# The last output projection: forms loaded as they stand in DRAM, half of it added to the residual by transfers, the last norm's rows fetched one product earlier

## The chip, the cores and the metric

The kernel runs on one core of a Trainium2 chip. The metric is the time of one execution in device microseconds (us), lower is better. Engines: PE (TensorE) multiplies matrices, ACT (ScalarE) and DVE (VectorE) work on elements, POOL (GpSimd) and SP (SyncE) issue transfers (DMAs). Sixteen DMA engines do the transfers of all queues. POOL issues the accumulating ones, which add to what stands at the target.

## The reference

Two layers on x of 512 rows x 2048 columns, all float32. The change is in the end of the second layer:

```python
def retention_branch(x, w_in, w_out):
    proj = jnp.einsum('bsd,de->bse', x, w_in)
    q, k, v, gate = jnp.split(proj, [...], axis=-1)
    ...                                   # rotary, chunkwise retention, 8 heads
    o = group_norm_heads(o).reshape(B, S, RET_V_WIDTH)      # 4096 wide
    y = o * jax.nn.silu(gate)
    return jnp.einsum('bse,ed->bsd', y, w_out)              # (4096, 2048)

    for i in range(DEPTH):                # layer 0: fox_branch, layer 1: retention_branch
        ...
        h = layer_norm(DEEPNORM_ALPHA * h + y, ln_gain[i], ln_bias[i])
```

## The kernel before

Products are taken with a scheme of seven products for eight quarter blocks (p1 to p7), on sums and differences of quarters. The activations' seven **forms** are called a11, a12, a22, s1, s2, s3, s4; `FORM` says which product uses which. The weights' sums are made on DVE (`w_q`, line 577). Each operand is split into a rounded part h (ACT, line 307) and the rest l (DVE, line 308), and a product is three matmuls (lines 312 to 314).

A **unit** is one projection of 1024 columns by 2048 rows of weights: 7 products of 4 blocks for a wide one, each block 12 matmuls. The last output projection is four units: 14 and 15 multiply the first 2048 of the 4096 columns of y, 16 and 17 the second 2048. `ORDER` and `EARLY` (unit 17) give the order of the products.

The program order on every engine is planned when the kernel is built, by the class `Order`. It goes from block to block (a **slot**; the planner counts 2.72 us for it) and lets **tasks** (generators) take steps between blocks. A step yields `need(...)`: its cost in DVE and ACT time, what it waits for, and tiles from rings, for instance `tmp=2`. Tasks of a lower rank come first. `give("tmp", 3)` returns a tile three slots later. The ring `tmp` has four tiles of 128 x 512.

The parts that the change touches:

- `retain()` is the end of a head. For the last head (7) its last loop makes four outputs y and -y, each in two `tmp` tiles, and `give_forms` (line 828) stores or accumulates them into the forms in DRAM, `yf[i]` (y_a, y_s in the profile). Then `given[1]` counts the head. It has rank 2.
- `fetch_forms` loads the forms of half i (1 for units 14 and 15, 2 for units 16 and 17) into `y_raw` and splits them. The loads wait for `given[1] >= 4 * i`. `fetch_while(2)` starts it while unit 15 runs: a11 when p5 is done, s1 when p6 is done, and so on.
- `residual` has written `ALPHA` times the first layer's normed result (gain and bias applied) to `z_res` in DRAM, 16 pieces of 128 x 512. `add_half` takes the sums of units 14 and 15: `loads_of` loads a piece of `z_res` into a `tmp` tile (line 1448, rank 1), DVE adds the unit's sum (line 1862), POOL stores it as `z_half` (line 1863). Units 16 and 17 load `z_half` and add their own sums (`add_z`, line 1472).
- A unit's sums stand in **kept** tiles (`keep`, line 425, copied out of PSUM by ACT): `hand` passes them on, for (0, 0), (0, 1) and (1, 1); the sum (1, 0) is passed on while it stands in its PSUM bank x. `after` has the additions and subtractions at products' ends (lines 460, 465, 470).
- `last_gains` fetches the last norm's gain and bias, each row of 512 spread over 128 partitions, 8 transfers of POOL (line 1885), one step each. In unit 17 POOL also accumulates weights (`v_sum`, line 493, after SP's load; `w_q`, line 613).

Of the kernel before, what the change touches and what calls it, by code (L numbers as in the profile page):

```python
# [11 lines left out]
F32 = mybir.dt.float32  # L12
F32R = mybir.dt.float32r
I32 = mybir.dt.int32
AF = mybir.ActivationFunctionType
ALU = mybir.AluOpType

P = 128
# [3 lines left out]
ST = S // P  # L22
# [36 lines left out]
EARLY = (("p1",), ("p5",), ("p2", "p6"), ("p3",), ("p7",), ("p4",))  # L59
# [30 lines left out]
class Order:  # L90
# [17 lines left out]
    def give(self, ring, after=0):  # L108
        if after:
            self.later.append((self.now + after, ring))  # L110
        else:
            self.free[ring] += 1
# [7 lines left out]
    def spawn(self, steps, rank=2):  # L120

        task = dict(steps=steps, last=self.now - 1, rank=rank)
        try:
            task["need"] = next(steps)
        except StopIteration:
            return
        at = sum(t["rank"] <= rank for t in self.tasks)
        self.tasks.insert(at, task)
# [99 lines left out]
def need(dve=0.0, act=0.0, pe=0.0, wait=1, until=lambda: True, **rings):  # L228
    return dict(dve=dve, act=act, pe=pe, wait=wait, until=until, rings=rings)
# [3 lines left out]
def trunk(ctx: ExitStack, tc: tile.TileContext, xq, x, fb_f, columns, wf_in, narrow, wide, ln_g, ln_b, rot, decay,  # L233
          out):
    nc = tc.nc
    home = dict(HOME)
    pool = ctx.enter_context(tc.tile_pool(name="sb", bufs=1))
    psum = ctx.enter_context(tc.tile_pool(name="ps", bufs=1, space=bass.MemoryType.PSUM))
    dram = ctx.enter_context(tc.tile_pool(name="dr", bufs=1, space=bass.MemoryType.DRAM))
    o = Order()  # L240
    spawn, take, give, free, require = o.spawn, o.take, o.give, o.free, o.require

    def f32(t):
        return t.bitcast(F32)
# [4 lines left out]
    def sb2(name):  # L249
        return pool.tile([P, 512], F32, name=name, tag="tmp", bufs=4)  # L250

    def tmp(name):
        take("tmp")
        return sb2(name)
# [50 lines left out]
    def split(src, h, l):  # L305

        nc.scalar.activation(h, src, AF.Copy)  # L307
        nc.vector.tensor_sub(l, src, f32(h))  # L308
# [8 lines left out]
    forms, ready = {}, {}  # L317

    def new_form(name):
        forms[name] = [pool.tile([P, 8, 256], F32R, name=name, tag=t) for t in home[name]]  # L320
        ready[name] = set()

    def split_form(name, src, k0, k1, es=slice(None), whole=True):
        split(src, *(t[:, k0:k1, es] for t in forms[name]))
        if whole:
            ready[name].update(range(k0, k1))
# [14 lines left out]
    def join_room():  # L341
        yield need(until=lambda: "room" in stock and free["y0"])
        stock.remove("room")
        take("st")
        take("y0")
        give("g2")
# [418 lines left out]
    def combine(rest, plain):  # L765
# [41 lines left out]
        for c in range(2):  # L807
# [7 lines left out]
    yf = [{f: dram.tile([P, 8, 256] if i == 0 else [P, 2, 8, P], F32, name=f"y_{f}{i}")  # L815
           for f in (("a11", "a12", "a21", "a22") if i == 0 else FORM.values())} for i in range(3)]
    z_norm = [dram.tile([P, D], F32, name=f"z_norm{s}") for s in range(ST)]
    z_res = {(s, c): dram.tile([P, 512], F32, name=f"z_res{s}{c}") for s in range(ST) for c in range(4)}
    z_half = {(s, c): dram.tile([P, 512], F32, name=f"z_half{s}{c}") for s in range(ST) for c in range(4)}


    given = [0, 0]
# [22 lines left out]
    VIA = {"a11": "s1", "s1": "s2", "s2": "s4", "s4": "s3", "s3": "a12", "a12": "a22"}  # L845
    passing = set()

    def fetch_forms(i, names):

        at = {}  # L850

        def loads():
            for n in names:
                if n not in VIA:
                    yield need(g0=1)
                    take("g0")
                t = pool.tile([P, 8, 256], F32, name="y_raw", tag=home[VIA[n]][0] if n in VIA else "g0")
                passing.add(VIA.get(n))
                for c in (0, 4):
                    yield need(wait=2, until=lambda: given[1] >= 4 * i)  # L860
                    for e in range(2):
                        nc.sync.dma_start(t[:, c:c + 4, e * P:(e + 1) * P], yf[i][n][:, e, c:c + 4])
                    at[n, c] = t, o.now

        spawn(loads(), 0)
        for n in names:
            for c in (0, 4):
                yield need(dve=1.14, act=0.97,
                           until=lambda: n not in passing and (n, c) in at and o.now - at[n, c][1] >= 4)
                if c == 0:  # L870
                    new_form(n)
                split_form(n, at[n, c][0][:, c:c + 4], c, c + 4)
            passing.discard(VIA.get(n))
            if n not in VIA:
                give("g0")

    def fetch_while(i):

        take = lambda *names: lambda: spawn(fetch_forms(i, names))
        return {"p5": take("a11"), "p6": take("s1"), "p7": take("s2", "s4"), "p4": take("s3", "a12", "a22")}  # L880
# [93 lines left out]
    class Pair:  # L974
# [13 lines left out]
        def take(self, m, n, tile, done):  # L988
            def copy():
                yield need(act=0.5, until=self.has_room)  # L990
                if self.raw is None:
                    self.new_raw()
                    self.new_sums()
                nc.scalar.activation(self.raw[m][:, :, n * 256:(n + 1) * 256], tile, AF.Copy)
                yield need(act=1.2)
                self.squares(m, n, tile, 0)
                done()
                self.have += 1

            spawn(copy(), 0)  # L1000
# [403 lines left out]
    def two_banks():  # L1404
# [5 lines left out]
        BOTH, then={len(BOTH) // 2 - 1: lambda: spawn(fetch("a21", "k2", "k0", "k1")), len(BOTH) - 1: late})  # L1410
# [28 lines left out]
    def loads_of(src, u, order, held):  # L1439

        got = {}

        def steps():
            for m, n in ORDERS[order]:
                for e in range(2):
                    yield need(tmp=1, until=lambda: len(got) < held and given[0] == FH)
                    t = tmp("z_in")
                    nc.sync.dma_start(t, src(2 * m + e, 2 * u + n))
                    got[m, n, e] = t, o.now

        return got, steps
# [128 lines left out]
    def last_banks():  # L1580
# [4 lines left out]
    sink, steps = add_z(0, ALPHA, x_rows, "plain", 2)  # L1585
    Plain(wide, 4, sink, last_banks).run(
        HELD, then={8: lambda s=steps: spawn(s(), 1)})
# [6 lines left out]
    sink, steps = add_z(1, ALPHA, x_rows, "each")  # L1594
# [249 lines left out]
    for h in heads[1:]:  # L1844
        if h.h == 2:
            spawn(biases())
        h.qk_unit.run(then={"p3": lambda h=h: spawn(h.attend())})
        then = fetch_while(1) if h.h == RH - 1 else {}
        last = then.get("p4", lambda: None)
        h.vg_unit.run(SLOW if h.h == 1 else ORDER, leaves=h.h == RH - 1,  # L1850
                      then={**then, "p4": lambda h=h, last=last: (spawn(h.retain()), last())})


    def add_half(u, held):
        got, steps = loads_of(lambda s, c: z_res[s, c], u, "order", held)

        def sink(m, n, tile, done):
            def add():
                for e in range(2):
                    yield need(dve=0.6, until=lambda: (m, n, e) in got and o.now - got[m, n, e][1] >= 2)  # L1860
                    t, _ = got.pop((m, n, e))
                    nc.vector.tensor_add(t, t, tile[:, e])
                    nc.gpsimd.dma_start(z_half[2 * m + e, 2 * u + n], t)
                    give("tmp", 3)
                done()

            spawn(add(), 0)

        return sink, steps

    sink, steps = add_half(0, 2)
    Unit(wide, 14, sink, u2="in1", p1="y0").run(then={"p6": lambda s=steps: spawn(s(), 1)})
    sink, steps = add_half(1, 2)
    Unit(wide, 15, sink, u2="k2").run(leaves=True, then={0: lambda s=steps: spawn(s(), 1), **fetch_while(2)})

    gb = []

    def last_gains():
        for i in range(2):
            gb.append(pool.tile([P, D], F32, name="ln_last", tag=home["a11"][i]))  # L1880
        for c in range(4):
            cs = slice(c * 512, (c + 1) * 512)
            for t, src in zip(gb, (ln_g, ln_b)):
                yield need()
                nc.gpsimd.dma_start(t[:, cs], src[1:2, cs].to_broadcast([P, 512]))

    def biases_there():

        yield need()
        nc.gpsimd.dma_start(row_b[0:1, 0:1], bf[0:1, :])  # L1890
        yield need(wait=4)
        nc.gpsimd.dma_start(bf[0:1, :], row_b[0:1, 0:1])
        yield need(wait=4)
        nc.vector.tensor_copy(bf[0:1, :], bf[0:1, :])
        fox["biased"] = True
# [26 lines left out]
    def last_stores(s):  # L1922
# [3 lines left out]
        for c in (0, 1, 3, 2):  # L1926
# [6 lines left out]
            else:  # L1933
                nc.gpsimd.dma_start(out[s * P:(s + 1) * P, cs], z, accum_op=ALU.add)

    half = lambda s, c: z_half[s, c]
    spawn(join_room(), 0)
    sink, steps = add_z(0, 1, half, "order")
    Unit(wide, 16, sink, u2="k2").run(then={0: lambda s=steps: spawn(s(), 1)})
    sink, steps = add_z(1, 1, half, "early")  # L1940
    Unit(wide, 17, sink, u2="k2").run(EARLY, then={0: lambda s=steps: (spawn(s(), 1), spawn(biases_there(), 0)), "p2": lambda: spawn(last_gains(), 0),
                                          "p3": lambda: [spawn(x) for x in (first_stores(), last_stores(2), last_stores(3))]}, last=True)
    o.flush()
    require(lambda: not o.tasks)
# [51 lines left out]
```

## Time and profile before

| what | us |
|---|---|
| median of 3 runs | 2376.63 |
| lowest and highest of them | 2374.23, 2378.85 |
| the profiled execution's own time | 2375.62 |
| its span, first to last instruction | 2373.9 |
| PE busy | 2305.4 |
| DVE busy | 1893.7 |
| ACT busy | 1214.0 |
| POOL busy | 166.0 |

The span is 1.7 us shorter than the execution's own time, as it leaves out what lies around the instructions. Lines of the profile name the engine, the line of the kernel and out<-in by the program's names; "PEld" is PE's load of weights, "SPq" SP's queue. Matmuls overlap, and their ends are modelled, so PE's busy time is a little too high.

### The profile page before, as it was taken

To read this page: it belongs to the slowest core of one execution; us is meant where nothing else is said; L and a number is where in the kernel's file an instruction comes from. 1 tells how busy PE (TensorE), PEld (TensorE's weight loads), DVE (VectorE), ACT (ScalarE), POOL (GpSimd) and SP (SyncE) were. 2 spreads that over 40 slices of the span, in tenths; PEclk is the share of its full clock that TensorE was granted. 3 is DMA by queue.
4 is the path that set the end of the run, shared out by engine and by line. 5 is a ranking of instruction groups with operands and counts; after the bars stand their busy time and mean duration, and the time that the engine had idled before them with its cause. 6 is when DMAs were issued, how large, how long until landed. Compare 5 with 4: busy or idle time off the path is not lost.

```text
span 2373.9 us, 32923 instructions
## 1 busy us (share of the span) xinstructions
PE 2305.4 (97%) x12424; PEld 1972.5 (83%) x12424; DVE 1893.7 (80%) x2477; ACT 1214.0 (51%) x1762; POOL 166.0 (7%) x256
## 2 busy tenths in 40 slices
PE   9999999989999999999999999999999999999995
PEld 9878778779899778888889898988888898777784
DVE  5887777777865655679889888888888889987977
ACT  4556656556554534565444545454545445554533
POOL 0000000000000000010010101010101001011002
PEclk9999999999999999999999999999999999999998
DMA  6355555455644457675585758575656659689778
GB/s 225 123 199 197 164 179 182 160 178 175 200 153 147 134 195 253 222 191 151 208 257 211 250 178 233 183 200 198 214 182 203 210 169 272 212 266 297 238 248 187
DMA packets 186350, 477.36 MB, mean 201 GB/s; under 512 B 18224, under 2 KB 63424, under 8 KB 185680
## 3 DMA queue, kind: packets, MB, share of 16 engines
q1 hardware_dynamic: 160288, 399.48, 50.2%
q0 software_dynamic: 25904, 75.78, 12.6%
q8 instruction: 97, 1.59, 0.3%
q14 instruction: 61, 0.50, 0.1%
HBM read 415.39 MB, written 64.00 MB: 202 GB/s over the span
## 4 chain that ended last, share of the span: by engine, by line
PE 61%; DVE 7%; DMA 4%; ACT 3%; issue 3%; SPq 0%; POOL 0%; DVEq 0%; ACTq 0%; POOLq 0%
PE acc L312 18%; PE acc L313 18%; PE acc L314 18%; DVE w_l L308 3%; DMA w_raw<-in_wide 2%; ACT w_h L307 2%; PE mmp L312 1%; PE mmp L313 1%; PE mmp L314 1%; DVE w_q L577 1%; PE mmp L1277 1%; DMA v_sum<-in_wide 1%; PE mmp L1800 1%; DMA y_raw<-y_a 0%; PE mmp L1132 0%
## 5 line engine op out<-in xcount | busy, mean ns | idle before, releaser
L307 ACT ACTIVATE w_h<-w_q 128x1024 fp32r<-128x1024 f32 x360 | 380.7, 1059 | 427.7 <-DVE w_q L577 229.6
L312 PE MATMUL acc<-w_h,a 128*128 128x512 f32 (+1 forms) x1440 | 535.5, 372 | 7.3 <-DVE kept L470 5.2
L308 DVE TENSOR_TENSOR w_l<-w_raw,w_h 128x1024 fp32r<-128x1024 f32 x314 | 383.6, 1222 | 190.8 <-ACT w_h L307 189.6
L313 PE MATMUL acc<-w_l,a 128*128 128x512 f32 (+1 forms) x1440 | 528.8, 367 | 5.2 <-DVE w_l L308 5.1
L314 PE MATMUL acc<-w_h,a 128*128 128x512 f32 (+1 forms) x1440 | 528.2, 367 | 0.0
L308 DVE TENSOR_TENSOR w_l<-w_q,w_h 128x1024 fp32r<-128x1024 f32 x360 | 439.6, 1222 | 107.4 <-ACT w_h L307 100.8
L307 ACT ACTIVATE w_h<-w_raw 128x1024 fp32r<-128x1024 f32 x314 | 331.8, 1058 | 363.2 <-PE acc L314 171.6
L313 PE MATMUL acc<-w_l,s 128*128 128x512 f32 (+1 forms) x1280 | 487.4, 381 | 9.8 <-DVE w_l L308 9.7
L312 PE MATMUL acc<-w_h,s 128*128 128x512 f32 (+1 forms) x1280 | 490.7, 383 | 0.4 <-ACT w_h L307 0.4
L314 PE MATMUL acc<-w_h,s 128*128 128x512 f32 (+1 forms) x1280 | 485.8, 380 | 0.0
L312 PEld LDWEIGHTS acc<-w_h,a 128*128 128x128 f32 x1440 | 272.0, 189 | 53.8 <-issue 9.6
L313 PEld LDWEIGHTS acc<-w_l,a 128*128 128x128 f32 x1440 | 272.3, 189 | 50.8 <-DVE w_l L308 10.2
L314 PEld LDWEIGHTS acc<-w_h,a 128*128 128x128 f32 x1440 | 271.9, 189 | 44.9
L313 PEld LDWEIGHTS acc<-w_l,s 128*128 128x128 f32 x1280 | 241.1, 188 | 59.7 <-DVE w_l L308 17.5
L314 PEld LDWEIGHTS acc<-w_h,s 128*128 128x128 f32 x1280 | 240.7, 188 | 45.4
L312 PEld LDWEIGHTS acc<-w_h,s 128*128 128x128 f32 x1280 | 241.0, 188 | 43.8 <-ACT w_h L307 0.9
L577 DVE TENSOR_TENSOR w_q<-w_q,w_raw 128x1024 f32<-128x1024 f32 x216 | 263.3, 1220 | 11.3 <-DMA w_raw<-in_wide 8.9
L314 PE MATMUL acc<-a,w_l 128*128 128x256 f32 x464 | 132.3, 285 | 1.7 <-DVE w_l L308 1.7
L312 PE MATMUL acc<-a,w_h 128*128 128x256 f32 x464 | 132.3, 285 | 1.5 <-ACT w_h L307 1.5
L313 PE MATMUL acc<-a,w_h 128*128 128x256 f32 x464 | 132.0, 284 | 0.0
L314 PE MATMUL acc<-s,w_l 128*128 128x256 f32 x448 | 126.8, 283 | 0.0
L313 PE MATMUL acc<-s,w_h 128*128 128x256 f32 x448 | 126.7, 283 | 0.0
(235 smaller groups left out, 2975.4 us busy)
## 6 DMA issues: line engine op xcount, KB each, us to landing
w_raw<-in_wide SPq DMA_DIRECT2D x364, 512.0 KB, 4.1
w_raw<-in_narrow SPq DMA_DIRECT2D x104, 512.0 KB, 3.7
w_q<-in_wide SPq DMA_DIRECT2D x72, 512.0 KB, 4.4
room<-in_wide SPq DMA_DIRECT2D x48, 512.0 KB, 4.3
y_s<-ny POOLq DMA_DIRECT2D x48, 256.0 KB, 7.1
y_s<-y POOLq DMA_DIRECT2D x40, 256.0 KB, 6.7
w_q<-in_narrow SPq DMA_DIRECT2D x18, 512.0 KB, 3.9
room<-in_narrow SPq DMA_DIRECT2D x18, 512.0 KB, 3.9
```

The lines of the kernel that those rows point to most:

```text
L307: nc.scalar.activation(h, src, AF.Copy)
L308: nc.vector.tensor_sub(l, src, f32(h))
L312: nc.tensor.matmul(ps, a[0], b[0], start=start, stop=False, skip_group_check=True)
L313: nc.tensor.matmul(ps, a[0], b[1], start=False, stop=False, skip_group_check=True)
L314: nc.tensor.matmul(ps, a[1], b[0], start=False, stop=stop, skip_group_check=True)
L577: nc.vector.tensor_add(u.chain[c], u.chain[c], t)
L1277: nc.tensor.matmul(ps[:, k * P:], vh[:, k], pT[:, k, k * P:], start=k == 0, stop=k == ST - 1)
L1800: nc.tensor.transpose(ps[t - 1][:, i], g[t - 1][:, i * P:(i + 1) * P], ident)
```

## The change

It does three things.

1. `fetch_forms`: the tile `y_raw` gets the order in which the forms of the retention layer stand in DRAM (half e, then k, then 128 columns). One transfer of 512 KB brings what two of 256 KB brought, in pieces of 2 KB where it was 512 bytes. The split reads the tile through a rearranged view and writes the same forms.
2. `add_half` has no loads and no additions on DVE: the kept tiles are accumulated onto `z_res` in DRAM by transfers of POOL. Only the sum in the bank (1, 0) is first copied by ACT to a `tmp` tile. `z_half` is gone, units 16 and 17 load `z_res`. Kept tiles are given back four slots after their transfers are issued.
3. `last_gains` is started after p1 of unit 17 instead of p2.

```diff
@@ fetch_forms
-                t = pool.tile([P, 8, 256], F32, name="y_raw", tag=home[VIA[n]][0] if n in VIA else "g0")
+                t = pool.tile([P, 2, 8, P], F32, name="y_raw", tag=home[VIA[n]][0] if n in VIA else "g0")
...
-                    for e in range(2):
-                        nc.sync.dma_start(t[:, c:c + 4, e * P:(e + 1) * P], yf[i][n][:, e, c:c + 4])
+                    nc.sync.dma_start(t[:, :, c:c + 4], yf[i][n][:, :, c:c + 4])
...
-                split_form(n, at[n, c][0][:, c:c + 4], c, c + 4)
+                split(at[n, c][0][:, :, c:c + 4].rearrange("p e k t -> p k e t"),
+                      *(t[:, c:c + 4].rearrange("p k (e t) -> p k e t", e=2) for t in forms[n]))
+                ready[n].update(range(c, c + 4))
@@ add_half
-    def add_half(u, held):
-        got, steps = loads_of(lambda s, c: z_res[s, c], u, "order", held)
+    def add_half(u):
         def sink(m, n, tile, done):
             def add():
                 for e in range(2):
-                    yield need(dve=0.6, until=lambda: (m, n, e) in got and o.now - got[m, n, e][1] >= 2)
-                    t, _ = got.pop((m, n, e))
-                    nc.vector.tensor_add(t, t, tile[:, e])
-                    nc.gpsimd.dma_start(z_half[2 * m + e, 2 * u + n], t)
-                    give("tmp", 3)
-                done()
+                    to = z_res[2 * m + e, 2 * u + n]
+                    if (m, n) == (1, 0):
+                        yield need(act=0.5, tmp=1)
+                        t = tmp("z_part")
+                        nc.scalar.activation(t, tile[:, e], AF.Copy)
+                        nc.gpsimd.dma_start(to, t, accum_op=ALU.add)
+                        give("tmp", 4)
+                    else:
+                        yield need()
+                        nc.gpsimd.dma_start(to, tile[:, e], accum_op=ALU.add)
+                done(0 if (m, n) == (1, 0) else 4)
             spawn(add(), 0)
-        return sink, steps
-    sink, steps = add_half(0, 2)
-    Unit(wide, 14, sink, u2="in1", p1="y0").run(then={"p6": lambda s=steps: spawn(s(), 1)})
-    sink, steps = add_half(1, 2)
-    Unit(wide, 15, sink, u2="k2").run(leaves=True, then={0: lambda s=steps: spawn(s(), 1), **fetch_while(2)})
+        return sink
+    Unit(wide, 14, add_half(0), u2="in1", p1="y0").run()
+    Unit(wide, 15, add_half(1), u2="k2").run(leaves=True, then=fetch_while(2))
@@ units 16 and 17
-    half = lambda s, c: z_half[s, c]
+    half = lambda s, c: z_res[s, c]
...
-    Unit(wide, 17, ...).run(EARLY, then={..., "p2": lambda: spawn(last_gains(), 0),
+    Unit(wide, 17, ...).run(EARLY, then={..., "p1": lambda: spawn(last_gains(), 0),
```

More of the change, by code (lines that the diff above doesn't have):

```diff
@@ L818, in trunk @@
     z_res = {(s, c): dram.tile([P, 512], F32, name=f"z_res{s}{c}") for s in range(ST) for c in range(4)}
-    z_half = {(s, c): dram.tile([P, 512], F32, name=f"z_half{s}{c}") for s in range(ST) for c in range(4)}
     given = [0, 0]
@@ L1940, in trunk @@
     sink, steps = add_z(1, 1, half, "early")
-    Unit(wide, 17, sink, u2="k2").run(EARLY, then={0: lambda s=steps: (spawn(s(), 1), spawn(biases_there(), 0)), "p2": lambda: spawn(last_gains(), 0),
+    Unit(wide, 17, sink, u2="k2").run(EARLY, then={0: lambda s=steps: (spawn(s(), 1), spawn(biases_there(), 0)), "p1": lambda: spawn(last_gains(), 0),
                                           "p3": lambda: [spawn(x) for x in (first_stores(), last_stores(2), last_stores(3))]}, last=True)
```

## The prediction

> **What bounds the kernel now.** I read the page first: busy time, then the chain that ended last.
>
> ```profile
> PE 2305.4 (97%) x12424; PEld 1972.5 (83%) x12424; DVE 1893.7 (80%) x2477; ACT 1214.0 (51%) x1762; POOL 166.0 (7%) x256
> PE 61%; DVE 7%; DMA 4%; ACT 3%; issue 3%; SPq 0%; POOL 0%; DVEq 0%; ACTq 0%; POOLq 0%
> ```
>
> TensorE is busy 97% of the span, so only its idle time, or work that it does not need to do, can be won. The change takes no matmul away. Next come the stretches of time around the last output projection (units 14 to 17). The columns are start and end, length, then busy us (and instructions) of PE, PEld, DVE, ACT and POOL, granted clock, share of the DMA engines, GB/s.
>
> ```profile
> 1960.00:2250.00 290.00, 282.70 (x1243) 229.31 (x1243) 255.45 (x266) 152.97 (x162) 25.75 (x39) 1.00 0.83 259
> 2040.00:2050.00 10.00, 8.95 (x38) 6.73 (x37) 9.93 (x10) 8.28 (x9) 0.00 (x0) 1.00 0.88 281
> 2080.00:2090.00 10.00, 8.63 (x40) 6.85 (x39) 9.79 (x17) 4.26 (x5) 0.54 (x1) 1.00 0.76 235
> 2130.00:2165.00 35.00, 34.99 (x158) 28.68 (x157) 23.15 (x20) 18.82 (x22) 7.86 (x10) 1.00 0.96 258
> 2160.00:2170.00 10.00, 7.31 (x32) 5.45 (x30) 7.85 (x8) 4.12 (x4) 0.57 (x1) 1.00 1.09 353
> 2165.00:2215.00 50.00, 45.60 (x196) 36.12 (x195) 46.39 (x45) 25.04 (x26) 5.44 (x10) 1.00 0.93 310
> 2200.00:2220.00 20.00, 18.29 (x77) 13.84 (x76) 18.65 (x18) 13.42 (x14) 1.59 (x3) 1.00 0.90 286
> 2280.00:2290.00 10.00, 10.00 (x46) 8.28 (x45) 8.64 (x9) 5.16 (x5) 0.00 (x0) 1.00 0.68 232
> 2290.00:2330.00 40.00, 38.46 (x167) 30.72 (x166) 24.31 (x24) 15.24 (x15) 9.79 (x13) 1.00 1.01 281
> ```
>
> The first row holds what can be won before the last unit: 290.00 - 282.70 = 7.3 us of PE idle. It sits in four places: 1.05 us in 2040:2050, 1.37 in 2080:2090, 2.69 in 2160:2170, 1.71 in 2200:2220. At three of them VectorE is nearly full (9.93 and 9.79 of 10, 18.65 of 20); at 2160 the DMA engines are (1.09). The clock is 1.00 throughout. The timeline of TensorE shows what such a wait really costs:
>
> ```profile
> 2040.45 0.40 PE L314 MATMUL acc<-w_h,a 128*128 128x512 f32 x1
> 2040.68 0.39 PE L312 MATMUL acc<-w_h,s 128*128 128x512 f32 x1
> 2041.74 0.50 PE L313 MATMUL acc<-w_l,s 128*128 128x512 f32 x1 [0.68 <-DVE w_l L308]
> ```
>
> Matmuls start 0.23 us apart, and this wait took 2041.74 - 2040.68 - 0.23 = 0.83 us where the row calls 0.68 idle. So each wait costs about 0.15 more than its idle time.
>
> The chain of waits names what ended the two waits at ends of units (start, length, what):
>
> ```profile
> 2087.20 0.60 DVE z_in L1862
> 2087.80 1.14 DVE kept L470
> 2089.08 0.47 PE acc L312
> ...
> 2154.67 11.58 DMA y_raw<-y_a
> 2166.33 1.07 ACT a L307
> 2167.42 1.23 DVE a L308
> 2168.65 1.14 DVE kept L470
> 2169.92 0.47 PE acc L312
> ```
>
> Both times TensorE waits for the subtraction of line 470, which empties the bank that p4 reuses. At 2087 an addition of the residual (line 1862) stands ahead of it on VectorE. At 2166 it is the split of form a11 for the last two units, whose load took 11.58 us.
>
> **The change part by part.**
>
> *Additions of the first half.* In the window 1900:2374, groups of instructions by line and form (busy, mean ns):
>
> ```profile
> L1862 DVE TENSOR_TENSOR z_in<-z_in,kept 128x512 f32<-128x512 f32 x10 | 6.7, 685 | 0.0
> L1804 ACT ACTIVATE y<-mmp 128x512 f32<-128x512 f32 x8 | 4.7, 585 | 0.0
> L308 DVE TENSOR_TENSOR qk_l<-rope,qk_h 128x1024 fp32r<-128x1024 f32 x2 | 2.4, 1220 | 0.0
> L308 DVE TENSOR_TENSOR s<-y_raw,s 128x1024 fp32r<-128x1024 f32 x16 | 19.5, 1220 | 1.7 <-ACT s L307 1.7
> ```
>
> Sixteen additions (10 of this row, 6 of sister forms) leave VectorE: 16 x 0.685 = 11.0 us. Four copies out of PSUM come to ScalarE at 0.585, the row of a copy of that size: 2.3 us, beside 25.04 busy of 50 us in 2165:2215, so they cost nothing; if that cover were gone, 0.6 us each. At 2087 the line 1862 piece lies directly ahead of line 470: -0.6 us, and I take that. The bounds are 0, if another task fills the slot, and -1.4, the whole idle time.
>
> *The temporaries.* This is the step the diff does not name. Ring tmp has four tiles. In add_half each residual piece holds one from its load until three slots after its addition; its loader has rank 1 and the last head's retain() rank 2, and retain() needs two tiles at once for each of its four outputs. POOL's and SP's timelines, then ScalarE's:
>
> ```profile
> 2104.91 0.54 POOL L828 DMA_DIRECT2D y_a<-y  x1 [5.10 <-ACT y L1804]
> ...
> 2130.80 0.55 POOL L828 DMA_DIRECT2D y_a<-y  x1 [5.85 <-ACT y L1804]
> ...
> 2147.21 0.57 POOL L828 DMA_DIRECT2D y_a<-y  x1 [5.12 <-ACT y L1804]
> ```
>
> ```profile
> 2112.97 0.88 SPq L1448 DMA_DIRECT2D z_in<-z_res  x2
> ...
> 2147.99 1.17 SPq L862 DMA_DIRECT2D y_raw<-y_a  x2
> ```
>
> ```profile
> 2131.37 1.04 ACT L425 ACTIVATE kept<-acc 128x1024 f32<-128x1024 f32 x1
> ```
>
> The first output leaves at 2104.91, the second only at 2130.80, the last at 2147.21, with loads of z_res between. Forms for the second half may be loaded only once retain() has finished (given[1] = 8), so their loads start at 2147.99, though p5 of unit 15, which calls for a11, was over by 2131.37. After the change no residual tile is held there. Retain() should then end some 40 us sooner, and a11 and s1 be loaded from about 2134 on. The accumulations of retain()'s outputs leave the crowded stretch before 2165 as well. VectorE is idle 35 - 23.15 = 11.9 us in 2130:2165, so three of the first four splits (3 x 1.22) fit there, and with the eight additions of unit 15 (5.5 us) some 9 us leave 2165:2215, where it is busy 46.39 of 50. The wait at 2166 goes: -2.7, and the waits of 2200:2220 go: -1.7; with 0.15 for each of four waits another -0.6. Bounds: 0 (the wait for line 470 stays behind other work) and -5.0 (all of it). I take the upper end, since both causes, the late load and the full VectorE, are removed at the place. What is late next there is the weights' own chain of w_q, w_h and w_l, which gets those 9 us of VectorE as slack.
>
> *Loads of forms.* DMA packets and issues of the same window, KB each, us to landing:
>
> ```profile
> DMA packets 61184, 111.78 MB, mean 236 GB/s; under 512 B 4708, under 2 KB 33380, under 8 KB 61156
> y_raw<-y_s SPq DMA_DIRECT2D x32, 256.0 KB, 5.9
> z_in<-z_half SPq DMA_DIRECT2D x16, 256.0 KB, 5.0
> ```
>
> 33380 - 4708 = 28672 packets are 512 B: 56 loads x 512. After, 28 loads in pieces of 2 KB, 256 packets each. The same list over the whole span has layer 0's form loads, 512 KB at once, and an accumulating transfer:
>
> ```profile
> w_q<-in_wide POOLq DMA_DIRECT2D x16, 512.0 KB, 5.4
> ...
> y_raw<-y_a SPq DMA_DIRECT2D x6, 512.0 KB, 4.9
> ```
>
> 4.9 us for 512 KB against two of 5.9 that share the queue: about 1 us sooner, and 28 issues fewer on SP. Where does it show? Only at 2040, where the load of unit 14's forms meets weights; VectorE there is full, so most of that wait stays: -0.4 of bounds 0 to -1.2. The split now reads pieces of 128 elements; the row qk_l<-rope, which reads such pieces, takes 1220 ns as s<-y_raw does: 0.
>
> The Trainium skill, DMA: Bandwidth & Descriptors, section Specifications, puts line rate at transfers of 512 B and more. By that the 512 B pieces lose nothing and this term would be 0, the sum 0.4 less. The trace speaks mildly against it: 256 KB in 512 B pieces took 5.9 us, in 2 KB pieces (z_in<-z_half) 5.0, though under different load.
>
> *Accumulating transfers, kept tiles.* Sixteen stores of z_half become accumulations onto z_res, and 16 loads go. An accumulation of 512 KB lands in 5.4 us (w_q's row above). Kept tiles come back four slots (10.9 us) later; the soonest reuse, k0 by unit 16's p1, is seven blocks (19 us) after p2's end. Cost 0; were POOL held up by over 10 us, ScalarE's copy of p1 would wait the rest. SP no longer has unit 15's z_res loads in its queue, and unit 16's loads go sooner. They take three of four tmp tiles, so the second copy of unit 15's p4 waits some four slots; its bank is due about twenty blocks on: 0.
>
> *The last norm's rows.* Eight transfers of 256 KB move from the end of unit 17's p2 to the end of its p1. When p1 ended, and what the rows met:
>
> ```profile
> 2280.10 1.03 ACT L425 ACTIVATE kept<-acc 128x1024 f32<-128x1024 f32 x1 [1.33 <-PE acc L314]
> ```
>
> ```profile
> 2325.93 0.91 POOL L1885 DMA_DIRECT2D ln_last<-in_ln_g  x1
> ```
>
> ```profile
> 2325.38 6.27 DMA v_sum<-in_wide
> ```
>
> Before, they were issued from 2325.93, behind the last v_sum accumulation; the DMA stage 2290:2330 (share 1.01) was nearly over. Now POOL can issue three or four at 2280, where the share is 0.68: 3.2 us of room, three transfers at 0.93 us (262 KB at 281 GB/s). The others follow POOL's first w_q accumulation, into the full stage: five x 0.93 = 4.7 us of delay for w_raw and v_sum at worst. TensorE idled 40 - 38.46 = 1.54 us there and works two blocks behind the splits, so part is hidden; and the last v_sum accumulation, 6.27 us with the rows behind it, may take 5.4 as w_q's: -0.9. Bounds -0.9 and +4.7; I take +1.0, nearer the low end because VectorE waits 15.7 us in that stage while TensorE waits 1.5.
>
> **Sum:** -0.6 - 2.7 - 1.7 - 0.6 - 0.4 + 1.0 = -5.0 us. The profiled execution took 2375.62 us, 1.0 below the median of the runs, 2376.63; the same gain gives 2370.6 and 2371.6.
>
> **The rivals.** 0.2% is 4.75 us, about what a measurement of this kernel can tell from no change.
> *The waits move.* VectorE's order is written out anew; what leaves 2165:2215 lets the planner put other splits there, and line 470 stays behind them. For it: VectorE is the releaser at every wait. Against: 11 us of work are really gone. Then only the 0.6 at 2087 and half of the 1.7 come, less the 1.0: 2376.2.
> *The rows collide* (the other side). None of the eight finds room, 8 x 0.93 = 7.5 us lands on v_sum's path, against gains of 6.0: 2378.1. It decides from the seventh transfer in the full stage on. For it: share 1.01. Against: 0.68 just before, and POOL has nothing ahead of the first three.
> The Trainium skill, DMA: Bandwidth & Descriptors, section Issuing engines are not separate DMA queues, supports it: POOL's transfers share the engines with SP's. The trace agrees as far as shares near 1 in 2290:2330 with both queues busy show.
> *Everything goes.* All 7.3 us idle and 1.2 for eight waits, the rows hidden: 2368.1.
>
> **How the numbers follow.** Forecast 0.58 (2368 to 2374, two thirds of it below 2371.9), the waits move 0.17, the rows collide 0.15, everything goes 0.10. Faster by over 0.2%: 0.39 + 0.10 = 0.49. Slower by over 0.2%: the collision with few of the gains, and what I do not see: 0.10. Within: 0.41. The range 2367 to 2377 leaves out the collision's upper part and the lowest tenth.
>
> **What would show it.** Right: four y stores of the last head close together before 2115; y_raw of a11 issued near 2134; no TensorE wait at 2166 nor at 2200 to 2215; y_raw in 2 KB packets landing under 5.5 us. Wrong: a wait for line 470 at the end of unit 15; the last v_sum accumulation taking longer than 6.27 us; TensorE idle over 2.5 us in 2290:2330.

## The result and the profile after

The changed kernel takes 2384.01 us (median of 11 runs, 2381.07 to 2389.07), the kernel before 2377.71 (11 runs beside them). The ratio is 1.0027 [1.0019, 1.0035]: 6.3 us slower. The profiled execution took 2381.36 us with a span of 2378.5, against 2375.62 and 2373.9 before; it is the second shortest of the 11, so its trace shows a little less of the loss than the median does.

First the page of the changed kernel: busy time by engine, and the shares of the chain that ended last.

```profile
PE 2306.5 (97%) x12424; PEld 1974.1 (83%) x12424; DVE 1884.2 (79%) x2461; ACT 1214.9 (51%) x1766; POOL 170.9 (7%) x256
PE 63%; DVE 8%; DMA 3%; ACT 3%; issue 2%; SPq 0%; ACTq 0%; POOL 0%; DVEq 0%; POOLq 0%
```

VectorE is 9.5 us less busy than before and POOL 4.9 more, as the change meant it. TensorE's busy time is no guide here: it rose by 1.1 us for the same 12424 matmuls. So I went to the same stretches as in the prediction, plus 2100:2115 (columns as there):

```profile
1960.00:2250.00 290.00, 284.22 (x1248) 231.57 (x1247) 246.96 (x251) 154.32 (x166) 30.30 (x38) 0.99 0.80 246
2040.00:2050.00 10.00, 8.98 (x38) 6.79 (x37) 9.92 (x10) 8.27 (x9) 0.00 (x0) 1.00 0.92 268
2080.00:2090.00 10.00, 9.77 (x47) 7.86 (x46) 9.79 (x16) 6.27 (x9) 3.15 (x4) 1.00 0.67 184
2100.00:2115.00 15.00, 11.10 (x41) 8.52 (x40) 6.10 (x6) 4.48 (x6) 6.30 (x8) 0.89 1.03 259
2160.00:2170.00 10.00, 10.00 (x46) 8.29 (x45) 9.19 (x10) 6.01 (x6) 1.78 (x2) 1.00 0.60 188
2165.00:2215.00 50.00, 49.67 (x219) 40.80 (x218) 43.48 (x38) 27.14 (x29) 7.52 (x9) 1.00 0.90 272
2200.00:2220.00 20.00, 19.67 (x87) 15.68 (x86) 18.60 (x17) 13.04 (x14) 0.00 (x0) 1.00 0.90 294
2280.00:2290.00 10.00, 10.00 (x46) 8.29 (x45) 8.38 (x9) 4.38 (x5) 1.55 (x3) 1.00 0.92 291
2290.00:2330.00 40.00, 33.27 (x134) 25.57 (x132) 19.13 (x19) 13.16 (x14) 9.15 (x13) 0.96 0.99 286
```

TensorE's idle time is down from 1.37 to 0.23 us in 2080:2090, from 2.69 to 0 in 2160:2170 and from 1.71 to 0.33 in 2200:2220. Two places stand against that. In the last rows' stage 2290:2330 the idle time went from 1.54 to 6.73 us, and in 2100:2115 TensorE is idle for 3.9 of 15 us, where the kernel before had no idle time:

```profile
2100.00:2115.00 15.00, 15.00 (x69) 12.41 (x69) 12.04 (x11) 7.62 (x9) 2.55 (x4) 1.00 0.91 279
```

**The new wait.** TensorE, ScalarE and POOL of the changed kernel, in order of time:

```profile
2105.47 0.39 PE L314 MATMUL acc<-w_h,a 128*128 128x512 f32 x1
2108.99 0.49 PE L312 MATMUL acc<-w_h,a 128*128 128x512 f32 x1 [3.13 <-ACT w_h L307]
2110.25 0.79 PE L313 MATMUL acc<-w_l,a 128*128 128x512 f32 x1 [0.77 <-DVE w_l L308]
2110.84 0.63 PE L314 MATMUL acc<-w_h,a 128*128 128x512 f32 x1
2111.27 0.63 PE L312 MATMUL acc<-w_h,a 128*128 128x512 f32 x1
...
2112.98 0.63 PE L313 MATMUL acc<-w_l,a 128*128 128x512 f32 x1
```

```profile
2100.70 0.60 ACT L1805 ACTIVATE y<-mmp 128x512 f32<-128x512 f32 x1 [2.14 <-DMA y_s<-y]
2107.40 0.60 ACT L1806 ACTIVATE ny<-mmp 128x512 f32<-128x512 f32 x1 [6.10 <-DMA y_s<-y]
2107.89 1.99 ACT L307 ACTIVATE w_h<-w_q 128x1024 fp32r<-128x1024 f32 x2
```

```profile
2086.38 1.79 POOL L1870 DMA_DIRECT2D z_res<-kept  x2 [56.90 <-DVE kept L465]
2088.63 0.86 POOL L1870 DMA_DIRECT2D z_res<-kept  x1 [0.47 <-DVE kept L470]
2089.24 0.81 POOL L827 DMA_DIRECT2D y_a<-y  x1
2091.72 0.88 POOL L827 DMA_DIRECT2D y_s<-y  x1 [1.66 <-issue]
2095.25 0.87 POOL L1870 DMA_DIRECT2D z_res<-kept  x1 [2.66 <-issue]
2096.92 0.57 POOL L827 DMA_DIRECT2D y_a<-y  x1 [0.80 <-ACT w_h L307]
2098.24 0.84 POOL L827 DMA_DIRECT2D y_s<-y  x1 [0.75 <-issue]
```

Read from the top down. TensorE waits for ScalarE's w_h. ScalarE could not split it, because ny (line 1806) stood ahead and waited 6.10 us for the transfer y_s<-y. ny writes a tmp tile that still holds an older y. The plan gives such a tile back three slots (8.2 us) after its use, but its store left POOL only at 2098.24. POOL's list says why: four accumulations of kept sums (line 1870) stand before and between the stores of the last head. That store's landing is the link in the chain of waits; the row of the accumulations, from the list of issues in 1900:2374 (KB each, us from issue to landing, the median), shows how slow such transfers are there:

```profile
2098.24 9.13 DMA y_s<-y
2107.89 1.06 ACT w_h L307
2108.97 1.24 DVE w_l L308
2110.25 0.79 PE acc L313
```

```profile
z_res<-kept POOLq DMA_DIRECT2D x10, 256.0 KB, 7.2
```

The price: between 2105.47 and 2110.84 three matmuls started where 0.23 us each were due, a loss of 5.37 - 3 x 0.23 = 4.7 us. After it the matmuls start 0.43 us apart (2110.84, 2111.27, and so on to 2112.98), six of them and part of a seventh: 1.3 more, and the granted clock is 0.89 in this window. Together 6.0 us.

**The last stage.** POOL's issues of the rows (line 1889) in the changed kernel, then the transfers in its chain of waits:

```profile
2279.32 0.59 POOL L1889 DMA_DIRECT2D ln_last<-in_ln_g  x1 [80.93 <-PE acc L314]
...
2281.06 0.55 POOL L1889 DMA_DIRECT2D ln_last<-in_ln_g  x1
2290.74 0.87 POOL L1889 DMA_DIRECT2D ln_last<-in_ln_b  x1
...
2307.65 1.11 POOL L1889 DMA_DIRECT2D ln_last<-in_ln_b  x1
```

```profile
2286.15 4.94 DMA w_raw<-in_wide
...
2292.37 7.34 DMA w_raw<-in_wide
...
2300.99 5.75 DMA w_raw<-in_wide
...
2311.97 17.18 DMA v_sum<-in_wide
...
2329.81 6.25 DMA v_sum<-in_wide
```

Three rows are out by 2281.06 and five follow into the full stage, as forecast. The chain of the kernel before has two w_raw loads here, and a shorter one of v_sum:

```profile
2291.79 6.15 DMA w_raw<-in_wide
...
2299.22 5.74 DMA w_raw<-in_wide
...
2310.19 14.56 DMA v_sum<-in_wide
```

The last v_sum accumulation leaves POOL at 2329.81, where it was 2325.38: 4.4 us later, though the copy at the end of this unit's p5 still came 0.9 us ahead (2290.10 against 2290.98). TensorE works behind these weights, so the lead is lost and more: 5.3 us in this execution.

### The profile page after: what moved, and what is told of

Same layout as the page of the kernel before. It is cut to its first block, busy times and chain, and to the rows that moved or that the text cites. A ratio compares the mean times of both kernels' runs of the same rounds, so it can differ in the third digit from the quotient of the medians.

```text
span 2378.5 us, 32822 instructions
## 1 busy us (share of the span) xinstructions
PE 2306.5 (97%) x12424; PEld 1974.1 (83%) x12424; DVE 1884.2 (79%) x2461; ACT 1214.9 (51%) x1766; POOL 170.9 (7%) x256
## 4 chain that ended last, share of the span: by engine, by line
PE 63%; DVE 8%; DMA 3%; ACT 3%; issue 2%; SPq 0%; ACTq 0%; POOL 0%; DVEq 0%; POOLq 0%
PE acc L313 19%; PE acc L312 19%; PE acc L314 19%; DVE w_l L308 3%; ACT w_h L307 2%; PE mmp L312 1%; PE mmp L313 1%; DMA w_raw<-in_wide 1%; PE mmp L314 1%; DVE w_q L577 1%; DMA v_sum<-in_wide 1%; PE mmp L1278 1%; PE mmp L1801 1%; PE mmp L1133 0%; DVE z L1904 0%
```

## The experiments

The theory: two costs, apart from each other. The rows cost the transfer engines' time for their bytes, about 7 us. The last head's stores, late behind the accumulations on POOL, cost 6 us. Against it stood that the rows are dear only because of what else was changed, that POOL's queue and not their bytes makes them dear, that three of them find room, and that the wait at 2105 comes from the count of slots alone.

**The rows back at p2, all else as changed.**

```diff
-"p1": lambda: spawn(last_gains(), 0),
+"p2": lambda: spawn(last_gains(), 0),
```

> The changed kernel with one part undone: the last norm's rows start after p2 of unit 17 again. Theory (two places): the rows in the full DMA stage cost 4.4 us or more of the last unit's time (its p7 subtraction went from 0.9 us ahead of before at p5 to 4.4 behind), so the time falls by 4 to 5.5 us from the changed kernel, to 2378.5 to 2380, and TensorE's idle time between p5 and p7 of unit 17 is that of before (about 2.5 us instead of 10). Rival (the accumulating transfers load the DMA engines and everything after is late, the rows are innocent): 2383 to 2385, as the changed kernel.

Measured: 2375.7 us, ratio to the kernel before 0.9997 [0.9988, 1.0006], so 0.0030 or 7.1 us better than the changed kernel, more than the 4 to 5.5 expected. The wait at 2105 is still there (2105.77 to 2108.85).

**The rows at p1 alone, in the kernel before.**

```diff
-"p2": lambda: spawn(last_gains(), 0),
+"p1": lambda: spawn(last_gains(), 0),
```

> The kernel before with this part of the change alone: the last norm's rows start after p1 of unit 17. Theory (two places): 4 to 5.5 us slower than before, 2381.5 to 2383.5, with v_sum's and w_raw's loads late between p5 and p7 of unit 17. Rival (the rows only hurt beside the accumulations of the changed kernel, or not at all): within 1 us of before.

Measured: 2384.4 us, 1.0031 [1.0020, 1.0043]: 7.4 us slower for this one word, again more than expected. Both ways give the rows some 7 us, so they do not need the rest of the change to cost that much. The windows of 2275:2340, the kernel before first, then this one:

```profile
2275.00:2340.00 65.00, 63.46 (x276) 51.12 (x274) 46.45 (x57) 27.39 (x27) 11.42 (x16) 1.00 0.92 267
2275.00:2340.00 65.00, 56.09 (x227) 43.91 (x226) 38.95 (x39) 22.42 (x23) 12.06 (x17) 0.95 0.91 261
```

TensorE does 7.4 us less in these 65 us, and the shares of the transfer engines are equal (0.92 and 0.91): the stage was full and stays full, it only lasts longer. From the copy at the end of p5 to the subtraction of line 470 after p7 it takes 58.1 us here (2293.12 to 2351.17), 49.5 before. A single execution thus shows 8.6 us, the changed kernel's 5.3, so the price is known to a few us only; the interval of the ratio is 4.8 to 10.2 us.

**The tmp tiles of the last head held seven slots, rows still at p1.**

```diff
-                    give("tmp", 3)
-                    give("tmp", 3)
+                    give("tmp", 7 if self.h == RH - 1 else 3)
+                    give("tmp", 7 if self.h == RH - 1 else 3)
```

> The changed kernel, where the last head's y and -y tiles come back to their ring seven slots after their use instead of three. Theory (two places): the new wait of ScalarE in unit 14 is for a y tile whose store has not landed when the planner already gives the tile out again; with seven slots it goes, and 4 to 5 us with it: 2379 to 2380. Rival (that wait of 4.7 us is hidden later, since VectorE sets the pace in units 15 and 16): under 1.5 us faster than the changed kernel, though the wait is gone.

Measured: 2376.99 us, 1.0002 [0.9993, 1.0011], a little more than expected.

**The sums accumulated only after retain(), tiles held three slots as before.**

```diff
-                        yield need()
+                        yield need(until=lambda: given[1] == RH)
                         nc.gpsimd.dma_start(to, tile[:, e], accum_op=ALU.add)
```

> The changed kernel, where the sums in kept tiles are accumulated onto the residual only once the last head's outputs have been issued, so that in unit 14 they stand behind its y stores in POOL's queue. If the wait for the y tile comes from POOL's queue being crowded by the four accumulations ahead of the y stores, the stores go out 2 to 6 us sooner, the wait shrinks from 4.7 us to under 2, and the time falls by 3 to 4.5 us from the changed kernel. If it comes from the early end of the outputs alone (four outputs in a row through four tiles), the wait stays within 1 us of 4.7 and the time too.

Measured: 2376.96 us, 1.0002 [0.9993, 1.0011]. The windows of 2080:2120 of the changed kernel, of the longer tiles and of the later sums, then POOL's list in the last:

```profile
2080.00:2120.00 40.00, 35.87 (x157) 28.81 (x156) 27.45 (x31) 20.50 (x27) 13.55 (x17) 0.96 0.95 255
2080.00:2120.00 40.00, 39.76 (x183) 32.69 (x183) 31.42 (x31) 22.11 (x27) 13.07 (x16) 1.00 0.98 265
2080.00:2120.00 40.00, 39.76 (x184) 32.70 (x183) 31.67 (x33) 23.16 (x30) 10.60 (x14) 1.00 0.92 255
```

```profile
2086.16 0.54 POOL L827 DMA_DIRECT2D y_a<-y  x1 [56.92 <-ACT y L1805]
2086.69 0.93 POOL L827 DMA_DIRECT2D y_s<-y  x1
2091.21 0.56 POOL L827 DMA_DIRECT2D y_a<-y  x1 [3.59 <-ACT y L1805]
```

Each edit alone takes the wait away, and each is worth 0.0025, 5.9 us, near the 6.0 counted in the trace. With the sums later, the stores of the first three outputs leave within a microsecond of their activations (those of the fourth, made at 2098.22, from 2103.74 on), and three slots are enough: ScalarE waits 1.23 us for a store where it waited 6.10, and TensorE waits there no longer. So it was the accumulations ahead of the stores on POOL that made the plan's three slots false. With longer tiles the stores are as late as before; the plan then puts the third output at 2106.88, and weights are split meanwhile.

**Both mended: rows at p2 with longer tiles, and rows at p2 with the sums after retain().** The edits are those above, put together.

> The changed kernel with both repairs: the last norm's rows after p2 again, and the last head's y tiles held for seven slots. Theory (two separate places, on top of gains that came as predicted): the two repairs add up, 1.0027 - 0.0030 - 0.0025 = 0.997, some 6 to 7.5 us faster than before, 2370 to 2372. Rival (the last unit's full DMA stage takes back what came sooner): 0.999 to 1.000, 2376 to 2378.

> The changed kernel with the rows after p2 again and the kept sums accumulated only behind the last head's y stores. Theory: the same 0.997, 2370 to 2372, as either repair takes away the same wait of ScalarE. Rival as for the kernel with rows and tiles: 0.999 to 1.000.

Measured: 2370.86 us, 0.9971 [0.9960, 0.9982], and 2370.87, 0.9973 [0.9963, 0.9983]. Both are faster than the kernel before and than the changed one. The two costs add: 1.0027 - 0.0030 - 0.0025 = 0.9972. So they are two causes.

**The 512 KB loads alone, in the kernel before.** The edit is the first part of the change, without the other two.

> The kernel before with the form loads of the change alone (512 KB at once, pieces of 2 KB, the split through a view). The prediction's term: -0.4 us, 2377.3; the wait at 2040 shrinks by up to half. By the Trainium skill's line (512 B is already line rate) exactly as before. A third possibility: the wait at 2166 too becomes shorter by 1 to 2 us, since the late load of a11 lands sooner there: 2375.5 to 2376.5.

Measured: 2376.25 us, 0.9998 [0.9990, 1.0006], no difference that shows. The wait did shrink, and at the place of the third possibility:

```profile
2160.00:2170.00 10.00, 9.18 (x41) 7.29 (x40) 9.52 (x10) 4.21 (x5) 0.57 (x1) 1.00 1.05 381
```

TensorE is idle for 0.82 us here instead of 2.69 (from start to start the wait is 1.20 us instead of 3.07), while 2040:2050 is as before (8.96 us busy, 8.95 before). The total did not follow. In this execution TensorE waits in the last unit from 2320.51 to 2323.41 and then starts eleven matmuls at half rate, where the kernel before waited from 2321.33 to 2322.16; whether every execution loses there what it won at 2166 is not shown. The loads in its list of issues, and in the changed kernel's:

```profile
y_raw<-y_s SPq DMA_DIRECT2D x16, 512.0 KB, 6.2
...
y_raw<-y_s SPq DMA_DIRECT2D x16, 512.0 KB, 5.6
```

One load of 512 KB takes about as long as one of 256 KB did (5.9), and half as many are issued.

**Four rows at p1, four at p2, in the kernel before.**

```diff
+    def last_gains(i, src):
...
-"p2": lambda: spawn(last_gains(), 0),
+"p1": lambda: spawn(last_gains(0, ln_g), 0), "p2": lambda: spawn(last_gains(1, ln_b), 0),
```

> The kernel before, where only the four transfers of the gain rows start after p1 of unit 17, the four of the bias rows after p2 as before. If there is room for three transfers at 2280 (share 0.68) as the prediction said, the cost is under 1.5 us against before. If each transfer issued before v_sum costs the same, wherever it goes, it is half of what all eight cost alone (1.0031): 3 to 4 us, 2380.7 to 2381.7.

Measured: 2380.25 us, 1.0011 [1.0003, 1.0020], 2.6 us. The interval, 0.7 to 4.8 us, holds half of the eight rows' 7.4 as well as one row past a room for three (0.9). It doesn't settle how much room there is at 2280.

**The rows at p1 issued by SP, in the kernel before.**

```diff
-                nc.gpsimd.dma_start(t[:, cs], src[1:2, cs].to_broadcast([P, 512]))
+                nc.sync.dma_start(t[:, cs], src[1:2, cs].to_broadcast([P, 512]))
```

and `"p1"` for `"p2"` as above.

> The kernel before with the rows after p1 of unit 17, but issued by SP instead of POOL. Theory (the bytes cost, through the 16 engines that all queues share): as costly as with POOL, 1.003, 2384, give or take 1.5. Rival (POOL's own queue costs: the rows stand between the accumulations of w_q and v_sum and make them issue late): within 1.5 us of before, 2376.5 to 2379.

Measured: 2383.63 us, 1.0024 [1.0015, 1.0033], 5.7 us; by POOL it was 1.0031 [1.0020, 1.0043]. POOL no longer has the rows in its queue, and most of the cost stays, so it does not come from what stands behind them on POOL. Now they stand between the weight loads of SP's queue, and that alone could make those late. The run with the rows on POOL answers this: SP's queue held no rows there, and its loads were late all the same. SP's loads of v_sum in 2280:2335, the kernel before and then the rows at p1 by POOL:

```profile
v_sum<-in_wide SPq DMA_DIRECT2D x4, 512.0 KB, 9.7
v_sum<-in_wide SPq DMA_DIRECT2D x4, 512.0 KB, 13.6
```

So rows that stand in one queue delay the transfers of the other; what the two queues share is the 16 engines. The Trainium skill, DMA: Bandwidth & Descriptors, section Issuing engines are not separate DMA queues, says the same, and these two ratios agree with it.

**The rows after p3, with the longer tiles.**

```diff
-"p2": lambda: spawn(last_gains(), 0),
-"p3": lambda: [spawn(x) for x in (first_stores(), last_stores(2), last_stores(3))]
+"p3": lambda: [spawn(last_gains(), 0)] + [spawn(x) for x in (first_stores(), last_stores(2), last_stores(3))]
```

> The kernel with both repairs (rows after p2, y tiles seven slots), with the rows still later, after p3 of unit 17. Theory (every row transfer issued before the last v_sum accumulation costs, every one behind it is free until VectorE needs it): as rows after p2 or up to 1 us faster, 2369.5 to 2371. Rival (then VectorE's multiplication with the gain waits for them at the end): 1 to 4 us slower, 2372 to 2375.

Measured: 2376.34 us, 0.9997 [0.9989, 1.0006], against 0.9971 with the rows at p2: 6 us lost again, at the other end, as the rival said and by more. The last matmul starts at 2345.45 with the rows at p2 and at 2345.55 with the rows at p3. VectorE has this wait only with the rows at p3:

```profile
DVE z L1904 <- DMA ln_last<-in_ln_g: 5.1, 1, 5.1
```

So TensorE ends at the same time, and then VectorE waits 5.1 us for a row of the gain. Of the three places tried, p2 is the one where the rows neither hold up the weights nor come late.

## Why the prediction was wrong

It said 2371.6 us, and the kernel takes 2384.01. Beside the kernel before in these runs that is +6.3 us where the sum had -5.0. Term by term:

- *Additions of the first half*, -0.6: right. From 2087.32 to 2089.08 TensorE started nothing before. Now the matmul behind this wait starts at 2088.28, 0.8 us sooner, and four transposes of the last head (line 1801, 0.4 us) stand in the gap; 0.23 us of idle time is left.
- *The temporaries*, the waits of 2166 and 2200, -4.4 with their restarts added: the waits went as forecast. Counted from start to start of the matmuls they had cost 2.8 and 2.2, and 0.5 is left. The last output y of the head is made at 2100.70 instead of 2146.23, 45 us sooner where "some 40" stood; the load of a11 comes at 2138, not 2134. VectorE was eased less than forecast: in 2165:2215 it is 2.9 us less busy (46.39 to 43.48), not 9, and in 2200:2220 as busy as before (18.60 and 18.65). Nor is the wait of 2166 this term's alone: the loads by themselves took 1.9 us of it. No run takes the two apart in the changed kernel.
- *Loads of forms*, -0.4: by themselves not to be told from 0 (0.9998 [0.9990, 1.0006]). "Only at 2040" was wrong: nothing changed there, and the wait of 2166 shrank, which the term before had already counted in full. That the loads would land under 5.5 us was wrong: 5.6.
- All these together are what the mended kernel has: 0.9971, -6.9 us [-9.5, -4.3]. The sum had -6.0 without the rows, and the gaps counted here come to 5.3, or 5.7 with the transposes.
- *Accumulating transfers, kept tiles*, "Cost 0": **this step failed**, by 6.0 us. It asked when the kept tiles come back and whether ScalarE's copies would wait for them. It did not ask what stands behind the accumulations on POOL. The step before had just moved the last head's stores to the same microseconds: it took retain()'s earlier end as a gain only, and its tiles' three slots as still true. The trace of before gave the size: POOL waited 5.1 to 6.3 us for each y, so a store left at once, and an accumulation of 512 KB landed in 5.4. In the changed kernel 256 KB took 7.2 us (the middle of ten), and the store that mattered 9.13.
- *The last norm's rows*, +1.0 of bounds -0.9 to +4.7: **the second failed step**, in its size: 7.4 us alone, about 7.1 within the change. Eight rows at 0.93 us are 7.5, so the price is near that of the rows' whole bytes at the stage's own rate, and the 15.7 us by which VectorE waits there hid little or none of it. That the two agree to 0.1 us is luck: the interval is 4.8 to 10.2, and part of the time is TensorE's half clock after its waits (twelve matmuls with the rows alone). The row I should have gone by is the share of 1.01: in that stage the time added was about the time lost. The upper bound is also below what was measured, since it took three rows out before it began; whether those three find room stays open. And the last v_sum accumulation did not get faster without the rows behind it, as the -0.9 had it: 6.25 us against 6.27.
- *Each wait costs 0.15 more than its idle time*: true for the short ones. The new wait cost another 1.3 us by the clock.

Without the two failed terms the sum is -6.0, which takes the profiled execution from 2375.62 to 2369.6; the mended kernel's took 2370.92. The rival *the rows collide* had the price about right (7.5), but set it against gains of 6.0 with nothing new in their way. The failed *Cost 0* made the gains vanish as well: -6.9 + 6.0 + 7.1 = 6.2, of the 6.3 measured.

## What to carry to other kernels

When a change makes a step end sooner, ask what it now meets: here the stores of the last head came into the same stretch of POOL's queue as the accumulations that replaced VectorE's work, and a fixed number of slots for giving a tile back was no longer true. A transfer put into a queue counts against what stands behind it, not only against its own tile. In a stage where the transfer engines' share was 1 and TensorE waited for weights, 7.5 us of moved bytes cost about 7 by POOL's queue and 5.7 by SP's; the place for them is where the chain neither loads weights nor waits for the bytes, and here that was found by trying one step earlier and one later.

## What was not expected of the hardware

The half clock after a wait (waits from start to start of the matmuls). In the kernel before, a wait of 3.07 us at 2166 was followed by matmuls at full rate, 0.23 us apart, and one of 3.21 us at 2339 by five that started 0.43 us apart; the granted clock is 0.76 in 2339:2346. With the rows at p1 alone TensorE started one matmul between 2328.90 and 2334.11, and twelve at half rate followed, 12 x 0.20 = 2.4 us more. The length does not decide it: with four rows at p1 a wait of 2.63 us (2168.53 to 2171.16) was followed five matmuls later by seven at half rate, and with the rows at p2 and the sums after retain() one of 3.37 us (2333.55 to 2336.92) by none. So a wait of some 3 us can cost 1 to 2.4 us beside its own length, or nothing.

The Trainium skill, TensorE: Matmul & The Clock Gate, section Part 1: The HAM clock gate (the "warmup" mystery), says that TensorE falls to half clock after at least one idle window of about 3.4 us, and that this window runs on whatever the kernel does. The trace agrees in the half rate (0.43 against 0.23), and a window that runs on by itself would let waits of like length differ as these did. It does not agree in the length, since half rate came after waits of 2.63 and 3.21 us; no run here shows the window itself.

POOL stands idle for 0.75 to 2.66 us between transfers in 2089:2099, for reasons that the profile calls "issue". Whether that, rather than the mere number of transfers ahead, delayed the stores was not tried.
